# Issuing both products of a PSUM bank ahead of the bank's readers, at four places of an encoder's attention

## The chip, the cores and the metric

The kernel runs on one core of one Trainium2 chip. The metric is the device time of one execution in microseconds (us); of several executions the median is given. Matmuls run on TensorE (PE in the profile, its weight loads PEld) and write to PSUM, eight banks of 128 x 512 float32. VectorE (DVE) and ScalarE (ACT) read the banks. SyncE (SP) issues the DMAs that bring weights from HBM; GpSimd (POOL) does little here.

## The reference

Two layers work on 256 tokens of width 2048. In each, one projection of the normed and modulated input feeds two kinds of attention side by side: four heads of differential attention and eight heads of latent attention (MLA). Both results go through one output projection, and an MLP of width 8192 follows. What the change touches is this:

```python
# differential attention, per head: two score maps, softmaxes, difference, values, norm
s = einsum('bhmqd,bhmkd->bhmqk', qi, kt) * scale
p = softmax(s + bias, axis=-1)
a = p[:, :, 0] - lam * p[:, :, 1]
o = einsum('bhqk,bhkd->bhqd', a, vt)
o = _rmsnorm(o, subln_g) * (1.0 - lambda_init)
# latent attention, per head: scores are a sum of two products
s = (einsum('bhqd,bhkd->bhqk', qn, knt) + einsum('bhqr,bkr->bhqk', qr, k_rope)) * scale
o = einsum('bhqk,bhkd->bhqd', softmax(s, axis=-1), vt)
# both: out_a, out_b side by side, times w_o
```

## The kernel before

All of w_in, w_o, the MLP's weights and w_ada stream from HBM once. A weight block of 128 x 2048 (1 MB) lands in one of five `raw` buffers; ACT rounds each half to a tile `hi` (line 151) and DVE computes the rest `lo` (line 154), so that three fast products (hi by hi, hi by lo, lo by hi) stand for one full-precision product. There are four `hi` and four `lo` buffers. The blocks of w_ada share the five `raw` buffers and are consumed by one DVE instruction of 128 x 2048 (line 380). SP issues each load when a `raw` buffer comes free, that is, behind a `lo` of line 154 or a line 380.

A framework builds the program. It orders each engine's instructions by priorities and its own estimate of when each can run, and puts semaphore waits where one engine reads what another wrote, or where two engines would touch the same PSUM bank. So the order in the source decides which accesses to a bank come first, and the framework fills the gaps on PE with products of the surrounding projections.

The attention of one layer works on tokens in two halves of 128 (`t` = 0 and 1), and each of these steps puts both halves into one bank:

- `diff_probs` (line 1242): for each of two score maps `m`, a product into `psc[:, t]` (line 1249) and then at once its reader on DVE (line 1250), which adds the bias and takes the row minimum. The ACT exponentials (line 1236) follow. There are 16 such banks in the two layers.
- `mla_steps.scores` (line 1311): for each half a sum of two products in `psm[:, t]` (lines 1315 and 1316) and at once its DVE reader (line 1317). `softmax_parts` (line 1232) does both exponentials and one reciprocal (line 1239), and line 1320 scales. Then `turn` transposes the result (line 1267). There are 16 such banks.
- `diff_steps.values` (line 1273): for each half two products into `po[:, t]` (line 1280) and at once a sum of squares on ACT (line 1284). Then a square root on ACT (line 1285), a reciprocal on DVE (line 1286) and the scaling into `o` on ACT (line 1289). There are 8 such banks.
- `diff_steps.turn` (line 1292): for each of two column halves two transposes into `pot[:, d]` (line 1298), and at once ACT's `do` (line 1300) and DVE's rest of it (line 1301). There are 8 such banks.

The products of these steps are float32, which the trace shows as two passes for each matmul; the transposes are one pass. Each layer first runs the projections, with the differential scores spread over them; then the value projection with the MLA heads spread over it (lines 296 to 298 of `tokens_by_k`); then the output projection's first column block (`rows_by_k`, lines 311, 312 and 314), whose four quarters of k have the values and turned outputs of the four differential heads between them: heads 0 and 1's values ahead of the first quarter, their turned outputs and heads 2 and 3's values between the first and the second, and heads 2 and 3's turned outputs between the second and the third.

Of the kernel before, what the change touches and what calls it, by code (L numbers as in the profile page):

```python
# [101 lines left out]
class Trunk:  # L102
# [1139 lines left out]
    def diff_probs(self, l, hd, q, k):  # L1242
        nc = self.nc
        ps_, rs = [], []
        for m in range(2):
            ps = self.bank("psc")
            s, mx = self.t("s"), self.s("mx")
            for t in range(2):
                nc.tensor.matmul(ps[:, t], q[:, m, t * P : (t + 1) * P], k[:, m], start=True, stop=True)
                nc.vector.tensor_tensor_reduce(  # L1250
                    s[:, t], ps[:, t], self.bias[:, hd, t], 1.0, 3.0e38, ALU.add, ALU.min, mx[:, t : t + 1]
                )
            rs.append(self.softmax_parts(s, mx))
            ps_.append(s)
        c1 = self.s("c1")
        nc.vector.tensor_scalar(c1, rs[1], self.lam[:, l : l + 1], None, ALU.mult)
        a = self.u("a")
        for t in range(2):
            nc.vector.tensor_scalar(ps_[1][:, t], ps_[1][:, t], c1[:, t : t + 1], None, ALU.mult)
            nc.vector.scalar_tensor_tensor(a[:, t], ps_[0][:, t], rs[0][:, t : t + 1], ps_[1][:, t], ALU.mult, ALU.subtract)  # L1260
        return a
# [8 lines left out]
    def diff_steps(self, l, hd, at, v, out):  # L1270
        nc = self.nc
        st = {}

        def values():
            po = self.bank("po")
            junk, tot, r = self.t("osq"), self.s("otot"), self.s("or")
            for t in range(2):
                for kt in range(2):
                    c = (hd % 2) * 256
                    nc.tensor.matmul(  # L1280
                        po[:, t], at[hd][:, kt, t * P : (t + 1) * P], v[hd // 2][kt][:, c : c + 256],
                        start=kt == 0, stop=kt == 1,
                    )
                nc.scalar.activation(junk[:, t], po[:, t], AF.Square, accum_out=tot[:, t : t + 1])
            nc.scalar.activation(r, tot, AF.Sqrt, bias=self.eps, scale=1.0 / 256.0)
            nc.vector.reciprocal(r, r)
            o = self.t("o")
            for t in range(2):
                nc.scalar.activation(o[:, t], po[:, t], AF.Copy, scale=r[:, t : t + 1])
            st["o"] = o  # L1290

        def turn():
            o = st["o"]
            pt = self.bank("pot")
            both = [self.parts("do") for _ in range(2)]
            for d, (hi, lo, _) in enumerate(both):
                for t in range(2):
                    nc.tensor.transpose(pt[:, d, t * P : (t + 1) * P], o[:, t, d * P : (d + 1) * P], self.ident)
                g = self.gl[:, l, d : d + 1]
                nc.scalar.activation(hi, pt[:, d], AF.Copy, scale=g)  # L1300
                nc.vector.scalar_tensor_tensor(lo, pt[:, d], g, hi.bitcast(F32), ALU.mult, ALU.subtract)
            out.extend(both)

        return values, turn

    def mla_steps(self, hm, qn, qr, kn, vm):
        nc = self.nc
        st = {}

        def scores():  # L1310
            ps = self.bank("psm")
            s, mx = self.t("sm"), self.s("mxm")
            for t in range(2):
                c = slice(t * P, (t + 1) * P)
                nc.tensor.matmul(ps[:, t], qn[hm // 2][:, hm % 2, c], kn[hm // 2][:, hm % 2], start=True, stop=False)
                nc.tensor.matmul(ps[:, t], qr[hm // 4][:, (hm // 2) % 2, c], self.kr[:, hm % 2], start=False, stop=True)
                nc.vector.tensor_scalar(s[:, t], ps[:, t], -1.0, None, ALU.mult, ALU.min, accum_out=mx[:, t : t + 1])
            r = self.softmax_parts(s, mx)
            for t in range(2):
                nc.scalar.activation(s[:, t], s[:, t], AF.Copy, scale=r[:, t : t + 1])  # L1320
            st["s"] = s

        def turn():
            st["t"] = self.transposed(st["s"])

        def values():
            if hm % 2 == 0:
                self.pom = self.bank("pom")
            for kt in range(2):
                c = (hm % 4) * P  # L1330
                v = vm[hm // 4][kt].rearrange("p a b -> p (a b)")
                nc.tensor.matmul(self.pom[:, hm % 2], v[:, c : c + P], st["t"][:, kt], start=kt == 0, stop=kt == 1)
            if hm % 2:
                self.mo += self.split(self.pom, "mo", True)

        return scores, turn, values


# [91 lines left out]
```

## Time and profile before

| | us |
|---|---|
| median of 3 executions (2177.63 to 2179.71) | 2178.62 |
| the profiled execution's own time | 2180.82 |
| its span, first to last instruction | 2178.8 |
| PE busy in the span | 2147.1 (99%) |
| PEld busy | 1860.6 (85%) |
| DVE busy | 1592.7 (73%) |
| ACT busy | 1143.1 (52%) |

The granted TensorE clock was 0.998 of full speed. The table is read like this: PE has work almost all the time, so a time can only become shorter by what PE waits for, or by what its instructions take. The attention of layer 0 lies at about 160 to 335 us of the span and that of layer 1 at about 1225 to 1395 us.

### The profile page before, as it was taken

What the parts mean: (1) busy time and instruction counts of PE and PEld (TensorE: products, weight loads), DVE (VectorE), ACT (ScalarE), POOL (GpSimd) and SP (SyncE); (2) the same over time, 40 slices, a digit from 0 to 9 for tenths busy, and PEclk for the clock granted to TensorE, in tenths of its full rate; (3) what the DMA queues carried; (4) which work ended last, traced back from release to release, by engine and by line L of the source; (5) the groups of instructions that cost most, each with busy time, mean ns of one, the idle gap of its engine ahead of it and who ended that gap; (6) DMA issues with size and microseconds to landing.
All of it is one profiled execution on the core that took longest, in us unless ns stands there. A gap on an engine that the chain in (4) does not pass through costs nothing.

```text
span 2178.8 us, 29359 instructions
## 1 busy us (share of the span) xinstructions
PE 2147.1 (99%) x11502; PEld 1860.6 (85%) x11502; DVE 1592.7 (73%) x2117; ACT 1143.1 (52%) x1725; POOL 6.8 (0%) x19
## 2 busy tenths in 40 slices
PE   7999999999999999999999999999999999999998
PEld 6899878898888888888889988888888888888886
DVE  7888878888688988888876876678555555555555
ACT  6555664565455355355454565546535534644643
POOL 0000000000000000000000000000000000000000
PEclk9999999999999999999999999999999999999999
DMA  9988889799888988888967665867655554555552
GB/s 385 423 339 328 329 337 336 274 339 338 322 321 323 351 315 332 312 335 320 336 223 278 254 222 217 288 223 262 245 194 179 207 194 174 193 206 181 193 195 95
DMA packets 87243, 594.75 MB, mean 273 GB/s; under 512 B 9857, under 2 KB 10305, under 8 KB 20289
## 3 DMA queue, kind: packets, MB, share of 16 engines
q1 hardware_dynamic: 85968, 587.08, 73.2%
q0 software_dynamic: 848, 5.28, 0.7%
q8 instruction: 90, 1.47, 0.3%
q10 hardware_dynamic: 288, 0.52, 0.1%
q14 instruction: 49, 0.39, 0.1%
HBM read 589.66 MB, written 3.18 MB: 272 GB/s over the span
## 4 chain that ended last, share of the span: by engine, by line
PE 94%; DVE 2%; DMA 2%; ACT 1%; issue 0%; SPq 0%; ACTq 0%
PE ps L217 19%; PE pr L314 13%; PE pr L311 13%; PE pr L312 13%; PE ps L220 10%; PE pk L260 3%; PE pk L284 2%; PE pk L194 2%; PE pk L198 2%; PE pk L197 2%; PE pv L296 1%; PE pv L297 1%; PE pv L298 1%; DMA raw<-in_w_o 1%; PE pk L281 1%; PE ps L197 1%
## 5 line engine op out<-in xcount | busy, mean ns | idle before, releaser
L154 DVE TENSOR_TENSOR lo<-raw,hi 128x1024 fp32r<-128x1024 f32 (+1 forms) x714 | 835.6, 1193 | 441.1 <-issue 221.1
L151 ACT ACTIVATE hi<-raw 128x1024 fp32r<-128x1024 f32 (+1 forms) x714 | 733.9, 1036 | 685.8 <-PE pr L312 368.1
L380 DVE SCALAR_TENSOR_TENSOR ada<-ada,cond 128x2048 f32<-128x2048 f32 x192 | 437.9, 2284 | 12.4 <-DMA ada<-in_w_ada 11.9
L217 PE MATMUL ps<-h,hi 128*128 128x512 f32 x1856 | 431.5, 390 | 0.0
L217 PEld LDWEIGHTS ps<-h,hi 128*128 128x128 f32 x1856 | 345.1, 188 | 69.5
L311 PE MATMUL pr<-hi,hid 128*128 128x512 f32 x1024 | 398.6, 389 | 0.0
L312 PE MATMUL pr<-hi,hid 128*128 128x512 f32 x1024 | 398.5, 389 | 0.0
L314 PE MATMUL pr<-lo,hid 128*128 128x512 f32 x1024 | 253.5, 389 | 0.0
L220 PEld LDWEIGHTS ps<-h,lo 128*128 128x128 f32 x1856 | 230.3, 192 | 4.5
L220 PE MATMUL ps<-h,lo 128*128 128x256 f32 x1856 | 231.7, 283 | 0.0
L314 PEld LDWEIGHTS pr<-lo,hid 128*128 128x128 f32 x1024 | 192.3, 188 | 39.9
L312 PEld LDWEIGHTS pr<-hi,hid 128*128 128x128 f32 x1024 | 192.3, 188 | 39.7
L311 PEld LDWEIGHTS pr<-hi,hid 128*128 128x128 f32 x1024 | 192.3, 188 | 39.6
L1192 ACT ACTIVATE sum<-ps 128x256 f32<-128x256 f32 x110 | 42.0, 383 | 114.7 <-PE ps L220 114.2
L194 PE MATMUL pk<-h,hi 128*128 128x256 f32 x320 | 90.4, 285 | 0.2 <-ACT h L705 0.2
L198 PE MATMUL pk<-h,lo 128*128 128x256 f32 x320 | 90.5, 283 | 0.0
L197 PE MATMUL pk<-h,hi 128*128 128x256 f32 x320 | 90.5, 283 | 0.0
L188 DVE TENSOR_TENSOR hid<-relu,hid 128x256 fp32r<-128x256 f32 x128 | 48.3, 420 | 49.6 <-ACT hid L187 49.6
L260 PE MATMUL pk<-hf,w 128*128 128x256 f32 x384 | 83.9, 379 | 0.0
L260 PEld LDWEIGHTS pk<-hf,w 128*128 128x128 f32 x384 | 72.7, 190 | 10.0 <-ACT hf L677 0.2
L194 PEld LDWEIGHTS pk<-h,hi 128*128 128x128 f32 x320 | 61.2, 192 | 0.6 <-ACT h L705 0.5
L198 PEld LDWEIGHTS pk<-h,lo 128*128 128x128 f32 x320 | 61.4, 192 | 0.2 <-DVE lo L154 0.2
(237 smaller groups left out, 2466.6 us busy)
## 6 DMA issues: line engine op xcount, KB each, us to landing
raw<-in_w_m SPq DMA_DIRECT2D x238, 1024.0 KB, 5.2
ada<-in_w_ada SPq DMA_DIRECT2D x192, 1024.0 KB, 6.3
raw<-in_w_o SPq DMA_DIRECT2D x32, 1024.0 KB, 6.7
raw<-in_w_m SPq DMA_DIRECT2D x24, 768.0 KB, 5.6
raw<-in_w_dv SPq DMA_DIRECT2D x16, 1024.0 KB, 5.0
raw<-in_w_t SPq DMA_DIRECT2D x12, 1024.0 KB, 4.9
w<-in_w_a SPq DMA_DIRECT2D x24, 384.0 KB, 13.5
raw<-in_w_a SPq DMA_DIRECT2D x12, 768.0 KB, 5.8
```

The costliest lines, as they stand in the source:

```text
L151: ins = self.nc.scalar.activation(hi, v, AF.Copy)
L154: ins = self.nc.vector.tensor_tensor(lo, v, hi.bitcast(F32), ALU.subtract)
L194: ins = mm(ps, hi, x[0], start=first, stop=False, skip_group_check=shared)
L197: mm(ps, hi, x[1], start=False, stop=False, skip_group_check=shared)
L198: self.last_mac = mm(ps, lo, x[0], start=False, stop=last, skip_group_check=shared)
L217: mm(ps.rearrange("p a b -> p (a b)"), part(w, k, 0), x[2], start=k == 0, stop=False)
L220: mm(ps[:, 0], part(w, k, 1), x[0], start=False, stop=k == nk - 1)
L260: self.nc.tensor.matmul(ps, v, whole[k], start=first, stop=last, skip_group_check=True)
L311: mm(ps, xh[:, c], part(i, 0), start=kq == 0 and i == 0, stop=False)
L312: mm(ps, xl[:, c], part(i, 0), start=False, stop=False)
L314: self.last_mm = mm(ps, xh[:, c], part(i, 1), start=False, stop=kq == 3 and i == 3)
L380: ins = nc.vector.scalar_tensor_tensor(w, w, 1.0, self.cond, ALU.mult, ALU.mult, accum_out=acc[:, i : i + 1])
```

## The change

In all four steps the readers move out of the loop that issues the products: both halves' products come first, then both halves' readers.

```diff
@@ diff_probs
             for t in range(2):
                 nc.tensor.matmul(ps[:, t], q[:, m, t * P : (t + 1) * P], k[:, m], start=True, stop=True)
+            for t in range(2):
                 nc.vector.tensor_tensor_reduce(
                     s[:, t], ps[:, t], self.bias[:, hd, t], 1.0, 3.0e38, ALU.add, ALU.min, mx[:, t : t + 1]
                 )
@@ diff_steps, values
                         po[:, t], at[hd][:, kt, t * P : (t + 1) * P], v[hd // 2][kt][:, c : c + 256],
                         start=kt == 0, stop=kt == 1,
                     )
+            for t in range(2):
                 nc.scalar.activation(junk[:, t], po[:, t], AF.Square, accum_out=tot[:, t : t + 1])
@@ diff_steps, turn
-            for d, (hi, lo, _) in enumerate(both):
+            for d in range(2):
                 for t in range(2):
                     nc.tensor.transpose(pt[:, d, t * P : (t + 1) * P], o[:, t, d * P : (d + 1) * P], self.ident)
+            for d, (hi, lo, _) in enumerate(both):
                 g = self.gl[:, l, d : d + 1]
                 nc.scalar.activation(hi, pt[:, d], AF.Copy, scale=g)
                 nc.vector.scalar_tensor_tensor(lo, pt[:, d], g, hi.bitcast(F32), ALU.mult, ALU.subtract)
@@ mla_steps, scores
                 nc.tensor.matmul(ps[:, t], qr[hm // 4][:, (hm // 2) % 2, c], self.kr[:, hm % 2], start=False, stop=True)
+            for t in range(2):
                 nc.vector.tensor_scalar(s[:, t], ps[:, t], -1.0, None, ALU.mult, ALU.min, accum_out=mx[:, t : t + 1])
```

No instruction is added or removed; the framework orders PE, DVE and ACT anew from this, while SP's order of loads stays as it was. In the rows below line numbers above 1249 are up to four higher in the changed kernel. Names carry the number of their tile.

On PE, in layer 0 at about 230 us, where the second MLA head's scores (`psm_2166`) meet the transposes of the first head's result (`pt_2182` from `sm_2094`); `pt_2159` belongs to a differential head:

```order
-L1267 MATMUL pt_2159<-ident,a_1753 128x128 x4
-L1315 MATMUL psm_2166<-kn_1848,qn_1969 128x256
-L1316 MATMUL psm_2166<-kr_1317,qr_2045 128x256
-L1267 MATMUL pt_2182<-ident,sm_2094 128x128
+L1268 MATMUL pt_2159<-ident,a_1753 128x128 x4
+L1318 MATMUL psm_2166<-kn_1848,qn_1969 128x256
+L1319 MATMUL psm_2166<-kr_1317,qr_2045 128x256
+L1318 MATMUL psm_2166<-kn_1848,qn_1969 128x256
+L1319 MATMUL psm_2166<-kr_1317,qr_2045 128x256
+L1268 MATMUL pt_2182<-ident,sm_2094 128x128 x4
 L194 MATMUL pss_2202<-lath_1402,hi_2191 128x256
```

Both halves of the second head's scores now stand ahead of the transposes.

On DVE at the same place before, with what each row waits for (the row minima of the first MLA head, `mxm_2095`, a w_ada block, the reciprocal of the first head's sums, `r_2103`):

```order
L1317 TENSOR_SCALAR sm_2094,mxm_2095<-psm_2093 128x256 [waits PE_49]
L380 SCALAR_TENSOR_TENSOR ada_2018,macc_80<-ada_2018,cond 128x2048 [waits DMAHW3_49]
L1317 TENSOR_SCALAR sm_2094,mxm_2095<-psm_2093 128x256 [waits PE_49]
L394 TENSOR_TENSOR mod_79<-macc_80,vec 128x2 [waits DVE_49]
L154 TENSOR_TENSOR lo_2192<-raw_2189,hi_2191 128x1024 [waits DMAHW6_49,Activation_49]
L1239 RECIPROCAL r_2103<-tot_2102 128x2 [waits Activation_49]
```

And in the changed kernel:

```order
L1321 TENSOR_SCALAR sm_2094,mxm_2095<-psm_2093 128x256 [waits PE_49]
L1321 TENSOR_SCALAR sm_2094,mxm_2095<-psm_2093 128x256
L380 SCALAR_TENSOR_TENSOR ada_2018,macc_80<-ada_2018,cond 128x2048 [waits DMAHW3_49]
L1239 RECIPROCAL r_2103<-tot_2102 128x2 [waits Activation_49]
L154 TENSOR_TENSOR lo_2192<-raw_2189,hi_2191 128x1024 [waits DMAHW6_49]
```

The two readers stand together ahead of the w_ada block, the first of them carries the wait on PE for the whole bank and the second none, and the reciprocal moved ahead of a `lo`.

On PE in layer 0 between the first and the second quarter of the output projection (at about 313 to 320 us; `pot` are turned outputs of heads 0 and 1, `po` values of heads 2 and 3), before, from the last product ahead of the second visit:

```order
L311 MATMUL pr_2817<-hi_2916,mo_2775 128x512
L1298 MATMUL pot_2858<-ident,o_2792 128x128 x2
L1298 MATMUL pot_2869<-ident,o_2807 128x128 x2
L1280 MATMUL po_2880<-v_2768,aT_2164 128x256
L1280 MATMUL po_2880<-v_2770,aT_2164 128x256
```

And in the changed kernel, right behind the first quarter:

```order
L1300 MATMUL pot_2858<-ident,o_2792 128x128 x4
L311 MATMUL pr_2817<-hi_2912,mo_2672 128x512
L312 MATMUL pr_2817<-hi_2912,mo_2672 128x512
L311 MATMUL pr_2818<-hi_2912,mo_2672 128x512
L312 MATMUL pr_2818<-hi_2912,mo_2672 128x512
L311 MATMUL pr_2817<-hi_2912,mo_2673 128x512
L1300 MATMUL pot_2869<-ident,o_2807 128x128
L1281 MATMUL po_2880<-v_2768,aT_2164 128x256
L1300 MATMUL pot_2869<-ident,o_2807 128x128 x3
```

Before, thirteen products of the second quarter stood between `pot_2858`'s first two transposes and `pot_2869`; now five stand between `pot_2858` and `pot_2869`. In layer 1 the same two `pot` banks now follow each other with none between.

On ACT at that place before (`hi_2972` and `hi_2976` are the halves of the weight block for the third quarter, `or` the root, `o` the scaled output):

```order
L1289 ACTIVATE o_2792<-po_2780,or_2783 128x256
L1284 ACTIVATE osq_2796,otot_2797<-po_2795 128x256
L151 ACTIVATE hi_2972<-raw_2970 128x1024 [waits DMAHW1_49,PE_49]
L1284 ACTIVATE osq_2796,otot_2797<-po_2795 128x256 [waits PE_49]
L151 ACTIVATE hi_2976<-raw_2970 128x1024
L1285 ACTIVATE or_2798<-otot_2797,eps 128x2 [waits Activation_49]
L1300 ACTIVATE do_2859<-pot_2858,gl 128x256 [waits PE_49]
L1289 ACTIVATE o_2807<-po_2795,or_2798 128x256 [waits DVE_49]
```

And in the changed kernel:

```order
L1291 ACTIVATE o_2792<-po_2780,or_2783 128x256
L1286 ACTIVATE osq_2796,otot_2797<-po_2795 128x256 x2
L151 ACTIVATE hi_2916<-raw_2910 128x1024
L1287 ACTIVATE or_2798<-otot_2797,eps 128x2 [waits Activation_49]
L151 ACTIVATE hi_2972<-raw_2970 128x1024 [waits DMAHW1_49,PE_49]
L1291 ACTIVATE o_2807<-po_2795,or_2798 128x256 [waits DVE_49]
L1291 ACTIVATE o_2807<-po_2795,or_2798 128x256
L1303 ACTIVATE do_2859<-pot_2858,gl 128x256 [waits PE_49]
```

`o_2807` moved ahead of one of the two conversions and ahead of `do_2859`; it still stands behind `hi_2972`, which waits for a weight block to land.

## The prediction

> **What bounds the kernel now.** I read the page first, for the shares and the chain of waits:
>
> ```profile
> span 2178.8 us, 29359 instructions
> PE 2147.1 (99%) x11502; PEld 1860.6 (85%) x11502; DVE 1592.7 (73%) x2117; ACT 1143.1 (52%) x1725; POOL 6.8 (0%) x19
> PE 94%; DVE 2%; DMA 2%; ACT 1%; issue 0%; SPq 0%; ACTq 0%
> ```
>
> PE is busy 99% of the span and carries 94% of the chain that ended last. A reader on DVE or ACT costs time only where PE stands still for it. Then the table by stage, with layer 0's attention and first output columns in the first row and layer 1's in the second:
>
> ```profile
> 155.00:345.00 190.00, 184.64 (x1072) 160.82 (x1072) 163.46 (x271) 111.17 (x219) 1.18 (x2) 1.00 0.87 323
> 1215.00:1440.00 225.00, 224.59 (x1266) 194.91 (x1265) 165.23 (x269) 130.01 (x240) 1.05 (x2) 1.00 0.69 250
> ```
>
> PE (the second number) is idle 190 - 184.64 = 5.36 us in layer 0 and 0.41 us in layer 1. So the whole prize is a few us of 2179. Then PE's own waits, with what ended them:
>
> ```profile
> PE pss L194 <- ACT hi L151: 2.1, 1, 2.1
> PE pss L198 <- DVE lo L154: 1.0, 2, 0.5
> PE pot L1298 <- DVE do L1301: 1.0, 1, 1.0
> PE pt L1267 <- ACT sm L1320: 0.9, 2, 0.5
> PE po L1280 <- ACT osq L1284: 0.5, 1, 0.5
> ```
>
> The first two are for weights. The fifth and the third are a product that waits for the bank's reader. The fourth is late because the second half's product was. Those three are what the change can move.
>
> **The change part by part.** No instruction is added or removed, so each term is a wait, or a seam between two kinds of products. First the unit prices, from the timeline of PE:
>
> ```profile
> 300.22 0.39 PE L297 MATMUL pv<-lo,h 128*128 128x512 f32 x1
> 301.36 0.39 PE L296 MATMUL pv<-hi,h 128*128 128x512 f32 x1
> 304.26 2.75 PE L1280 MATMUL po<-v,aT 128*128 128x256 f32 x12
> 306.85 0.27 PE L1104 MATMUL pg<-ident,mod 128*16 128x128 f32 x1
> ```
>
> Five wide products from 300.22 to 301.36 are 0.227 us each; twelve float32 passes from 304.26 to 306.85 are 0.216.
>
> *The first MLA head's softmax, both layers.* PE, DVE and ACT in layer 0, then PE in layer 1:
>
> ```profile
> 230.38 0.60 PE L1267 MATMUL pt<-ident,a 128*128 128x128 f32 x4
> 230.82 0.60 PE L1315 MATMUL psm<-kn,qn 128*128 128x256 f32 x2
> 231.25 0.59 PE L1316 MATMUL psm<-kr,qr 128*128 128x256 f32 x2
> 232.39 0.33 PE L1267 MATMUL pt<-ident,sm 128*128 128x128 f32 x1 [0.55 <-ACT sm L1320]
> 226.97 2.28 DVE L380 SCALAR_TENSOR_TENSOR ada<-ada,cond 128x2048 f32<-128x2048 f32 x1
> 229.18 0.42 DVE L1317 TENSOR_SCALAR_CACHE_REDUCE sm<-psm 128x256 f32<-128x256 f32 x1
> 231.82 0.91 ACT L1320 ACTIVATE sm<-sm,r 128x256 f32<-128x256 f32 x2
> 1291.32 0.59 PE L1316 MATMUL psm<-kr,qr 128*128 128x256 f32 x2
> 1292.30 0.33 PE L1267 MATMUL pt<-ident,sm 128*128 128x128 f32 x1 [0.38 <-ACT sm L1320]
> ```
>
> PE's two passes from 231.25 end their turn at 231.68, and the transposes start at 232.39: 0.71 us lost; in layer 1, 1292.30 - 1291.32 - 0.43 = 0.55 us. The second reader at 229.18 stood behind a w_ada block of 2.28 us. In the new order it is ahead of the block, the reciprocal comes right behind the block, and the second head's other four passes (0.86 us) stand ahead of the transposes. So PE would ask for `sm` at 232.55 while ACT can scale it from about 230.4: both waits go, **-1.26 us**. The cover that hides what remains of this chain is those 0.86 us and the value projection ahead of it; if it is gone, the old 1.26 stay (bounds -1.26 to 0). What is moved past is the w_ada block, 0.42 us later on DVE, for which PE does not wait. The pairs of later heads show no wait on PE at all.
>
> *The last differential head in layer 0, at 203 us.*
>
> ```profile
> 202.44 1.82 PE L1249 MATMUL psc<-k,q 128*128 128x256 f32 x6
> 204.24 0.39 PE L194 MATMUL pss<-lath,hi 128*128 128x256 f32 x1
> 205.93 0.38 PE L198 MATMUL pss<-lath,lo 128*128 128x256 f32 x1 [0.51 <-DVE lo L154]
> 204.65 2.36 DVE L154 TENSOR_TENSOR lo<-raw,hi 128x1024 fp32r<-128x1024 f32 x2
> ```
>
> Six passes are 1.30 us and took 1.80 to the next product, so 0.50 is lost, and the last two passes of the second map come later. In the new order all eight passes run at once (1.73 us). But the first reader now waits for both halves (its wait on PE stands for the bank), so the first `lo`, which stands behind both readers, comes hardly earlier than at 204.65. The second `lo`, which stood directly behind the first, now has the other map's two readers ahead of it (0.42 us each, as the row at 229.18 has it for the other kind), and came only just in time at 207.01 (204.65 + 2.36). So the 0.50 won are about the 0.84 that the second `lo` comes later, less what the first gives. I take **0** (bounds -0.7 to +0.7).
>
> *Values and turned outputs in layer 0.* PE, then ACT, then the chain of waits:
>
> ```profile
> 311.31 0.84 PE L314 MATMUL pr<-lo,mo 128*128 128x512 f32 x3
> 312.69 1.13 PE L1280 MATMUL po<-v,aT 128*128 128x256 f32 x4 [0.54 <-ACT osq L1284]
> 317.12 0.39 PE L311 MATMUL pr<-hi,mo 128*128 128x512 f32 x1
> 318.49 0.82 PE L1298 MATMUL pot<-ident,o 128*128 128x128 f32 x4 [0.98 <-DVE do L1301]
> 311.43 0.84 ACT L1289 ACTIVATE o<-po,or 128x256 f32<-128x256 f32 x2 [0.26 <-DVE or L1286]
> 306.13 8.14 DMA raw<-in_w_o
> 314.35 1.06 ACT hi L151
> ```
>
> Gone: 312.69 - 311.31 - 3 x 0.227 = 0.70 and 318.49 - 317.12 - 0.23 = 1.14, together 1.84 us. Late next is the second head's `o`. PE runs 16 passes from 304.26 (to 307.7), 24 wide products (5.45, to 313.2), `pot_2858` (four transposes, 0.44 by the rows 230.38 and 230.82) and five wide products: it asks for `o` of the second head at 314.8. ACT has that behind a conversion whose block lands at 306.13 + 8.14 = 314.27, so conversion until 315.4 and half of `o` by 315.8: PE waits 1.0 us. By the same count the fourth head's `o` is about 0.3 late. Net **-0.5** (bounds: -1.84 if nothing is late; +1.6 if each of the two places waits for one more conversion of 1.06 on top of the 1.3 counted). SP's order of loads stays, but DVE's second `lo` of the second quarter waits for a conversion that is now behind `o`, about 3 us later than before, and with it the next load's issue; at that time two blocks are still on the way, which covers it.
>
> *The same in layer 1.*
>
> ```profile
> 1364.53 2.75 PE L1280 MATMUL po<-v,aT 128*128 128x256 f32 x12
> 1374.56 0.83 ACT L1289 ACTIVATE o<-po,or 128x256 f32<-128x256 f32 x2
> ```
>
> Here PE waited for nothing. Now the two `pot` banks follow each other: the first at 1364.53 + 3.46 + 5.45 = 1373.4, the second 0.44 later, at 1373.9. ACT's second `o` began at 1374.56; in the new order the two conversions of the next block stay ahead of it, and one sum of squares and the first `do` are not between them any more. I put it at 1374.0: half of it is there at 1374.4 and the rest at 1374.85, and PE's transposes, which take the halves in turn, wait some **+0.8** in all (bounds 0, and +2.1 with two more conversions of 1.06).
>
> *Seams.* Wide products behind a group of float32 passes run a little slower for a while:
>
> ```profile
> 250.67 0.59 PE L1315 MATMUL psm<-kn,qn 128*128 128x256 f32 x2
> 252.92 0.39 PE L297 MATMUL pv<-lo,h 128*128 128x512 f32 x1
> ```
>
> From 250.67 to 252.92 stand four passes and six wide products: 0.86 + 1.36 = 2.22, and it took 2.25, 0.03 us more. By the order, 47 such groups stand among the wide products of both attentions before and 25 in the changed kernel: 22 x 0.03 = **-0.7** (bounds 0, if the slower pace goes with the passes and not with the seam, and -1.5 at twice the price).
>
> Sum: -1.26 + 0 - 0.5 + 0.8 - 0.7 = **-1.7 us**. The profiled execution took 2180.82 and would take 2179.1; the median of the three runs was 2178.62, 2.2 below it, and goes to **2176.9**.
>
> A rule speaks against the change. ACT's second read of a bank that DVE reads in between shows that readers, too, take turns:
>
> ```profile
> 306.47 0.39 ACT L187 ACTIVATE mo<-pom 128x256 fp32r<-128x256 f32 x1 [0.68 <-DVE mo L188]
> ```
>
> The Trainium skill, Perfetto Trace Analysis, section Matmuls, says that independent groups of products should go to different banks in turn, so that emptying one overlaps the next group's products. By that rule a bank that is filled whole before anybody reads it gives up the overlap inside it, and the first reader starts later by the second half's products. This is the mechanism of the second rival below.
>
> **The rivals.** *All waits go and nothing comes back* (faster). For it: the three reader waits are each ended by one late reader, and the framework's own order believes `o` is ready when it puts `pot` early. Against it: the landing at 314.27 does not depend on the order of the attention. It gives -1.26 - 0.7 - 1.84 - 0 - 0.7 = -4.5: 2174.1. Chance 0.15.
>
> *Filling the bank first delays the chain behind it* (slower). The first reader of a value bank starts four passes (0.86 us) later, and ACT takes root, conversions and `o` one after the other behind it; PE now reaches the four second-of-pair `pot` banks early and waits there. It decides where `o` is more than about 1 us behind PE. The longest wait of PE for a conversion in this trace is 2.1 us (for `pss`, above); at four places that is 8.4, against 1.26 + 0.7 + 1.84 + 0.7 = 4.5 gained: +3.9, 2182.5. For it: o behind a conversion at each. Against it: in layer 1 loads land early. Chance 0.12.
>
> *The change does nothing that counts* (same). The load stream is the bound where the largest wait goes:
>
> ```profile
> 310.00:315.00 5.00, 4.46 (x21) 3.43 (x20) 3.75 (x6) 3.01 (x7) 0.49 (x1) 1.00 0.99 347
> ```
>
> DMA engines are busy 0.99 there, so what PE gains before is waited for again at the next block. Then only the MLA heads' 1.26 counts, less layer 1's 0.8: 2178.2. Against it: PE's idle time in this row, 5.00 - 4.46 = 0.54, is the wait for `osq` alone, none of it for weights. Chance 0.15.
>
> The Trainium skill, PSUM, section PSUM bank collisions raise a hardware error, has it that no two engines may touch one bank at once, readers included. The row at 306.47 agrees (0.68 us); it leaves ACT's and DVE's turns on `pot` as they are, and by it none of `pot`'s waits between those two would go.
>
> **How the numbers follow.** A change of 0.2%, 4.4 us, is about what a measurement of this kernel tells from none. The forecast has 0.58. Faster by more than 4.4 needs nearly the whole first rival: 0.08 with the forecast's tail. Slower by more needs the second rival's far end: 0.07. Same: 0.85. The range holds the forecast's bounds where one or two terms fall to an end (2.8 lower with nothing late in layer 0, 1.3, the seams' far end, 0.8, and 0.7 at 203 us; 3.4 higher with both `o` terms at their high ends, 2.1 and 1.3) and most of the rivals: 2174.0 to 2180.4.
>
> **What would show it.** In the changed profile: no wait of `pt` on `sm` and of `po` on `osq`; a wait of `pot` on ACT's `o` at about 314.8 of some 1 us, and one of under 1 us in layer 1; PE's idle time in 155 to 345 about 1 to 2 us smaller. Wrong would be: `pt` still waiting, `pot` waiting over 2 us, or new waits for weights between 330 and 400.

## The result, and the profile after

The changed kernel takes 2174.91 us (median of 14 executions, 2173.39 to 2176.31). The kernel before, run beside it, takes 2179.31 us (14 executions, 2177.63 to 2182.14). The ratio is 0.9979 with a 95% interval of 0.9971 to 0.9987: 4.4 us less, between 2.8 and 6.3. A later comparison of the same two kernels gave 0.9985 (0.9976 to 0.9994), 3.3 us less. The forecast was 1.7 us less. The sign and the range held; what follows is mostly about the 1.6 to 2.7 us that the forecast did not have.

The page of the changed kernel:

```profile
span 2172.8 us, 29358 instructions
PE 2144.7 (99%) x11502; PEld 1863.5 (86%) x11502; DVE 1590.9 (73%) x2117; ACT 1139.8 (52%) x1725; POOL 6.8 (0%) x19
```

PE's busy time fell by 2.4 us although it runs the same instructions. So a part of what went was counted as busy before. PE's own waits:

```profile
PE pss L194 <- ACT hi L151: 2.1, 1, 2.1
PE pss L198 <- DVE lo L154: 0.7, 2, 0.5
PE pr L311 <- ACT hi L151: 0.7, 2, 0.4
```

The three waits for a bank's reader (`pot` on `do`, `pt` on `sm`, `po` on `osq`) are gone. The last of these lines, the waits for blocks of `w_o`, was longer before:

```profile
PE pr L311 <- ACT hi L151: 2.4, 3, 1.0
```

These 1.7 us cannot be put down to the change: over the traces of the experiments these waits lie between 0.7 and 3.0 us, the 3.0 in a kernel with all readers behind their products and 1.0 in one whose layer 0 is that of before. The stretches of the two attentions, in the same columns as before:

```profile
155.00:345.00 190.00, 187.10 (x1077) 164.91 (x1076) 162.33 (x271) 110.07 (x219) 1.18 (x2) 0.98 0.85 322
1215.00:1440.00 225.00, 225.00 (x1267) 197.64 (x1266) 167.37 (x273) 130.21 (x243) 1.05 (x2) 1.00 0.71 254
```

PE is idle 2.90 us in layer 0 instead of 5.36, and not at all in layer 1, where it had been idle 0.41. By this table layer 1 can have given no more than 0.41 us. Two fixed points say otherwise. They are the first product of layer 0's MLP and the first of layer 1's; between them lies all of layer 1's attention. Timeline of PE before:

```profile
410.75 0.62 PE L194 MATMUL pk<-h,hi 128*128 128x256 f32 x3 [0.24 <-ACT h L705]
1465.67 0.62 PE L281 MATMUL pk<-h,lo 128*128 128x256 f32 x3 [0.24 <-ACT h L705]
```

And in the changed kernel:

```profile
407.79 0.62 PE L194 MATMUL pk<-h,hi 128*128 128x256 f32 x3 [0.24 <-ACT h L705]
1459.86 0.62 PE L281 MATMUL pk<-h,lo 128*128 128x256 f32 x3 [0.24 <-ACT h L705]
```

This stretch took 1054.92 us and now takes 1052.07, **2.85 us less**. Layer 1, for which my terms sum to about nothing (-0.55 + 0.8 - 0.3), gave more than half of the whole gain. The two profiled executions differ by 6.1 us, more than the medians do; of that, 3.0 us lie ahead of the first point (410.75 to 407.79) and 0.2 us behind the second.

**What the busy share hid.** Here is one place in layer 1 before the change, at the first half and second half of one score bank; all engines, rows of ACT and of other instructions left out:

```profile
1236.72 0.40 DVE L1250 CUSTOM_DVE_ANT_0 s<-psc,bias 128x256 f32<-128x256 f32 x1
...
1236.89 0.28 PE L198 MATMUL ps<-h,lo 128*128 128x256 f32 x1
1237.05 0.08 DVE L1250 DVE_READ_ACCUMULATOR2_ANT mx<- 128x1 f32 x1
1237.18 0.30 PEld L1249 LDWEIGHTS psc<-k,q 128*128 128x128 f32 x2 [0.21 <-DVE mx L1250]
1237.18 0.70 PE L1249 MATMUL psc<-k,q 128*128 128x256 f32 x2
...
1237.53 0.47 PE L194 MATMUL ps<-h,hi 128*128 128x256 f32 x1
...
1237.84 0.28 PE L197 MATMUL ps<-h,hi 128*128 128x256 f32 x1
```

The fast products (`ps`) start every 0.12 us. The product after 1236.89 was due at 1237.01 and started at 1237.18: its weights could be loaded only once the first half's reader had ended, at 1237.05 + 0.08 = 1237.13. From 1237.18 to 1237.84 stand two passes (0.43) and one fast product (0.12), 0.55, and it took 0.66. The wait cost 0.17 + 0.11 = 0.28 us. PE's row carries no idle time for it, because the bar of the product at 1236.89 is 0.28 long, more than the 0.12 from one start to the next, and covers the gap. PEld's row does carry it, 0.21. The same place in the changed kernel, PE:

```profile
1236.62 1.89 PE L1249 MATMUL psc<-k,q 128*128 128x256 f32 x8
1238.16 0.47 PE L194 MATMUL ps<-h,hi 128*128 128x256 f32 x1
1238.47 0.28 PE L197 MATMUL ps<-h,hi 128*128 128x256 f32 x1
```

Eight passes and one fast product from 1236.62 to 1238.47 are 1.85 us, exactly 8 x 0.216 + 0.12.

So the view that I should have read is the table of waits of PEld, here for 1215 to 1440 us before:

```profile
PEld psm L1315 <- DVE sm L1317: 0.9, 4, 0.3
PEld po L1280 <- ACT osq L1284: 0.9, 3, 0.3
PEld pqr L1222 <- ACT qr L346: 0.8, 1, 0.8
PEld pt L1267 <- ACT sm L1320: 0.8, 1, 0.8
PEld pt L1267 <- issue: 0.5, 2, 0.3
PEld pot L1298 <- ACT o L1289: 0.4, 2, 0.2
PEld psc L1249 <- ACT k L346: 0.2, 1, 0.2
PEld psc L1249 <- DVE mx L1250: 0.2, 1, 0.2
```

And of the changed kernel:

```profile
PEld pqr L1222 <- ACT qr L346: 0.8, 1, 0.8
PEld pt L1268 <- issue: 0.5, 2, 0.3
```

Of these waits PE's own view held one, `pt` on `sm`. The table tells which reader was waited for, and not what it cost: `psc` has 0.4 us in it, of two waits, and by the starts of the products lost 1.14 us; `psm` has 0.9 and lost 0.50. The Trainium skill, Perfetto Trace Analysis, section Identifying the Most-Contended Engine, says that the busy share of matmuls is not a good measure of how close a kernel is to its roofline, because matmuls are pipelined, and names the busy share of the weight loads as one of two to use instead. This case agrees: with PE at 224.59 of 225.00 us busy before, and 225.00 after, the stretch between the fixed points still became 2.85 us shorter, while PEld's busy time went from 194.91 to 197.64.

To compare all kernels I summed, from the starts of PE's passes, what each entry into and step inside a group (products of one kind that follow each other) took beyond its pace (0.216 us for a pass, 0.109 for a transpose), in layer 1. The last column is the stretch between the two fixed points.

| kernel | `psc` | `psm` | `pt` | `po` | `pot` | stretch |
|---|---|---|---|---|---|---|
| before, two traces | 1.14, 1.15 | 0.50, 0.51 | 0.56, 0.57 | 0.48, 0.48 | 0.11, 0.12 | 1054.92, 1054.86 |
| changed, two traces | 0.09, 0.09 | 0.00, 0.00 | 0.01, 0.01 | 0.00, 0.00 | 0.01, 0.01 | 1052.07, 1052.08 |

Layer 1 repeats to 0.1 us from one execution to the next. Layer 0 does not, as the experiments show.

### The profile page after: what moved, and what is told of

Read it like the earlier page. It is cut to its first block, busy times and chain, and to the rows that moved or that the text cites. A ratio compares the mean times of both kernels' runs of the same rounds, so it can differ in the third digit from the quotient of the medians.

```text
span 2172.8 us, 29358 instructions
## 1 busy us (share of the span) xinstructions
PE 2144.7 (99%) x11502; PEld 1863.5 (86%) x11502; DVE 1590.9 (73%) x2117; ACT 1139.8 (52%) x1725; POOL 6.8 (0%) x19
## 4 chain that ended last, share of the span: by engine, by line
PE 97%; DVE 2%; DMA 1%; ACT 0%; SPq 0%; issue 0%; ACTq 0%
PE ps L217 19%; PE pr L312 13%; PE pr L311 13%; PE pr L314 13%; PE ps L220 10%; PE pk L260 3%; PE pk L284 2%; PE pk L194 2%; PE pk L198 2%; PE pk L197 2%; PE pv L298 2%; PE pv L296 2%; PE pv L297 2%; PE pk L281 1%; PE ps L198 1%; PE ps L197 1%
```

## The experiments

Theory A: the gain out of sight is short waits of a bank's second product on the first one's reader. Theory B: it is the groups of other products, of which the changed kernel has fewer, each at a price. Later runs ask which layer the gain lies in.

**One part at a time.** Each of four kernels has one of the four edits of the diff and nothing else.

```diff
@@ diff_probs (first kernel)
+            for t in range(2):
                 nc.vector.tensor_tensor_reduce(...)
@@ mla_steps, scores (second kernel)
+            for t in range(2):
                 nc.vector.tensor_scalar(s[:, t], ps[:, t], -1.0, ...)
@@ diff_steps, values (third kernel)
+            for t in range(2):
                 nc.scalar.activation(junk[:, t], po[:, t], AF.Square, ...)
@@ diff_steps, turn (fourth kernel)
+            for d in range(2):
+                for t in range(2):
+                    nc.tensor.transpose(pt[:, d, ...], o[:, t, ...], self.ident)
             for d, (hi, lo, _) in enumerate(both):
```

> Only the differential scores (psc) get both products ahead of the readers; the rest is as before. Theory A, short waits: in the trace of before the first pass of a bank's second half starts 0.05 us after the first half's reader ends, and it and the pass behind it take 0.1 to 0.3 us longer than passes elsewhere; the table of waits does not list these. Summed over the start-to-start times of PE they are 0.5 us in layer 0 and 1.06 us in layer 1. A expects these sums to fall to under 0.1 each and the time to fall by 1.6 us to about 2177.7. Theory B, seams: the same time was lost at each change between kinds of products; layer 1 lost 2.05 us more than its one listed wait, over 28 groups that are fewer in the changed kernel, 0.073 us each. Here 15 groups go: -1.1 us, 2178.2, with the short waits of psm, po and pot smaller too if they belong to groups. Theory C, my prediction's own account: nothing at 203 us and 0.03 a seam, -0.45 us, 2178.9.

> Only the MLA scores (psm) get both products ahead of the readers. Both A (short waits) and my prediction expect the two waits of pt on sm to go, 0.71 us in layer 0 and 0.55 us in layer 1. A adds the short waits of psm, 0.1 us in layer 0 and 0.5 us in layer 1: -1.85 in all, 2177.5. B (seams at 0.073 us, 16 groups fewer) gives -1.26 - 1.17 = -2.4: 2176.9. The prediction's price of 0.03 gives -1.26 - 0.48 = -1.74. The traces should tell: under A the entries into psm cost nothing any more while entries into psc, po and pot cost what they did.

> Only the values (po) get both products ahead of the squares. A: the listed wait on osq in layer 0 (0.70 us and 0.10 for the pass behind it) and short waits of 0.17 in layer 0 and 0.48 in layer 1 go, -1.4 us in all; in layer 0 part of it may be waited for again at weights at 375 us. 2177.9. B: 3 groups fewer at 0.073 and the listed wait: -0.9. The prediction's mechanism of a late o would show as a longer wait of pot.

> Only the turned outputs (pot) are issued ahead of their readers. A: the listed wait on do in layer 0 (1.14 us) and some 0.3 us of short waits go, and as nothing of the values moves, the second head's o is as late as before, so pot waits for o: by the prediction 1.0 us in layer 0. So A expects -0.5 to -1.4: 2177.9 to 2178.8. If pot does not wait for o, the prediction's term of +1.3 in layer 0 was wrong without the values' help; if it does, the change of the values is what keeps o in time in the full change.

Measured against before (2178.95, 33 executions), and in layer 1 of the trace:

| only | time, us | ratio (95%) | `psc` | `psm` | `pt` | `po` | `pot` | stretch, less than before |
|---|---|---|---|---|---|---|---|---|
| `psc` | 2177.85 | 0.9992 (0.9983 to 1.0001) | 0.09 | 0.51 | 0.56 | 0.45 | 0.12 | 1.06 |
| `psm` | 2177.74 | 0.9994 (0.9985 to 1.0003) | 1.14 | 0.00 | 0.01 | 0.44 | 0.12 | 1.26 |
| `po` | 2177.94 | 0.9994 (0.9985 to 1.0003) | 1.17 | 0.51 | 0.56 | 0.01 | 0.22 | 0.40 |
| `pot` | 2179.40 | 1.0001 (0.9992 to 1.0010) | 1.16 | 0.51 | 0.56 | 0.29 | 0.24 | 0.17 |

None of the four is told from no change by its time. By the medians each gave less than A expected (1.1 us for 1.6, 1.2 for 1.85, 1.0 for 1.4, and 0.4 more for 0.5 to 1.4 less); their sum is 2.9 us less. The traces tell them apart. Each edit takes away the waits of its own kind and leaves the others: with `psc` alone, PEld's waits in 1215 to 1440 us are these, all of before but the two on `psc`:

```profile
PEld psm L1316 <- DVE sm L1318: 0.9, 4, 0.3
PEld po L1281 <- ACT osq L1285: 0.9, 3, 0.3
...
PEld pt L1268 <- ACT sm L1321: 0.8, 1, 0.8
...
PEld pot L1299 <- ACT o L1290: 0.4, 2, 0.2
```

With `psm` alone, `psm` and `pt` are gone and the rest stands:

```profile
PEld po L1280 <- ACT osq L1284: 0.9, 3, 0.3
...
PEld pot L1298 <- ACT o L1289: 0.4, 2, 0.2
PEld psc L1249 <- ACT k L346: 0.2, 1, 0.2
PEld psc L1249 <- DVE mx L1250: 0.2, 1, 0.2
```

The four stretches sum to 2.89 us against 2.85 for the whole change, so in layer 1 the parts add up. Theory A gave 1.06 for `psc` and got 1.06. In layer 0 the second head's `o` was late for `pot` with the values alone (PE waited 0.3 us for it), and not with the turned outputs alone, against my expectation. In layer 1 the edit of the turned outputs is worth little by itself, and it does not stand alone: with `po` batched and `pot` not, `pot` waits for `do` (0.22 instead of 0.11), and only both together bring it to 0.01. In layer 1 each of the two edits of the scores leaves eight groups fewer, so B's 0.073 us a group would have given `psc` and `psm` 0.58 us each beside `pt`; without `pt` the stretches give 1.06 and 0.70, and the single places lose 0.08 to 0.28 each, which is no one price for each group.

**Groups back, waits not.** The changed kernel, with the second halves' products issued later but still ahead of both readers:

```diff
@@ tile_cols
             self.mac(ps, w[k // per], (k % per) * m, m, xs[k], k == 0, k == nk - 1)
+            if k in (3, 6) and self.held:
+                self.held.pop(0)()
@@ diff_probs: the products of t = 0 at once; held (heads 0 to 2), one for each map:
+            product(m, 1)
             for t in range(2):
                 nc.vector.tensor_tensor_reduce(...)
```

> The changed kernel, but the second half's differential scores (psc) of heads 0 to 2 are issued three and six blocks into the next column, still ahead of both readers. PE then has 10 groups of psc in layer 1 instead of 4 (and 6 instead of 4 in layer 0), as before the change, but no product waits for a reader of its own bank. A (short waits on the first half's reader): a seam without such a wait costs nothing; the sum of what PE loses at the entries into psc in layer 1 stays at 0.1 us as in the changed kernel, where it was 1.14 us with the readers between, and the time stays at that of the changed kernel, about 2174.9. B (seams at 0.073 us): layer 1 gets 0.44 us longer and layer 0 0.15. My prediction's price of 0.03 would give 0.18 and 0.06.

The sum for `psc` in layer 1 is 0.12 us, the stretch 1052.06, and the time 2175.03 (0.9984, 0.9976 to 0.9993) beside 2175.57 for the changed kernel on the same chip. Six more groups in layer 1 cost 0.03 us together, where theory B gives 0.44 and my price of 0.03 for each 0.18: both are refuted. (The trace is of a long execution, 2178.97 us. What made it long lies ahead of the stretch; in layer 0 PE waited 3.0 us for blocks of `w_o`.)

**The wait taken away by another bank.** The order of the source as before, a bank for each half:

```diff
@@ diff_probs
-            ps = self.bank("psc")
             s, mx = self.t("s"), self.s("mx")
             for t in range(2):
+                ps = self.bank("psc")
@@ mla_steps, scores: the same with "psm"
```

> The kernel before, readers in their old place in the source, but each half of psc and of psm has a bank of its own, so the second product has no reader to wait for. po and pot as before. A: the same waits go as with the two changes of the scores alone: in layer 1 psc from 1.14 to 0.1, psm from 0.50 to 0, pt from 0.56 to 0, 2.3 us together (1.07 and 1.27 by those two runs from the same point to the same point), po and pot unchanged at 0.6. If it is not the wait on the bank but the place of the readers on VectorE that counts (both behind both products, ahead of a block of w_ada), psc and psm keep part of their loss here. If filling a bank before anybody reads it costs something, this kernel is faster than those two runs together, since its first reader starts a product earlier.

`psc` 0.09, `psm` 0.00, `pt` 0.01, `po` 0.44, `pot` 0.13; the stretch is 2.13 us shorter, against 1.06 + 1.26 = 2.32 for the two single edits. The time is 2176.23 (0.9987, 0.9978 to 0.9995). Of PEld's waits in the changed steps in layer 1, those on `po` and `pot` alone are left:

```profile
PEld po L1280 <- ACT osq L1284: 0.9, 3, 0.3
...
PEld pot L1298 <- ACT o L1289: 0.4, 2, 0.2
```

So what counted is that the second product had to wait for a reader of its own bank. Where the readers stand matters little: of `psc`, `psm` and `pt` together 2.1 us went here, as in the two single edits. A first reader that may start a product earlier brings nothing either, since the stretch did not become shorter than those two give. That it is 0.2 us longer than their sum shows in no wait of the table. My prediction held against the change a rule of the Trainium skill (Perfetto Trace Analysis, section Matmuls: let independent groups go to different banks). Both ways of keeping that wait away, two banks or one bank filled first, take away the same waits of the scores here; for the scores, filling one bank first has cost nothing that a run shows.

**Both kernels once more.**

> The kernel before once more, for a second trace. Layer 1 should repeat to 0.1 us: psc 1.14, psm 0.50, pt 0.56, po 0.48, pot 0.11 us. Layer 0 is the question: in the first trace PE waited 2.4 us for halves of w_o between 375 and 395 us, in the traces of the single parts only 0.7 to 1.0. If that belongs to the execution and not to the kernel, this trace has about 1 us there too, and the 3 us by which layer 0 differed between the first two traces were partly chance.

> The changed kernel once more, beside the others on one chip, and a second trace. About 2174.9 us. Layer 1 should repeat to 0.1 us; in layer 0, what PE waits for weights may change by a microsecond either way.

The kernel before took 2178.72 us in one execution, the changed one 2175.57 (ratio to before 0.9985, 0.9976 to 0.9994). Layer 1 repeats, as the table above shows. Layer 0 does not: from the last product of the setup, at 83 us, to the first of the MLP it took 327.43 and 325.83 us before, and 324.47 and 321.89 in the changed kernel. My expectation was not met: what PE lost to waits for halves of `w_o` between 345 and 410 us is the same 3.1 us in the second trace of before. (The kernel with the edits in layer 1 alone, below, whose layer 0 is that of before, lost 1.4 there, so it does vary.) What changed between the two traces is what my prediction counted as gone, the waits of PEld in 155 to 345 us. The first trace of before:

```profile
PEld pot L1298 <- DVE do L1301: 1.8, 2, 1.4
...
PEld po L1280 <- ACT osq L1284: 1.0, 1, 1.0
```

And the second:

```profile
PEld po L1280 <- ACT osq L1284: 0.4, 1, 0.4
PEld pot L1298 <- DVE do L1301: 0.4, 1, 0.4
```

Some two thirds of these two waits, 2.0 of 2.8 us, belonged to that one execution. The 2.6 us between the two traces of the changed kernel are of another kind, the clock of PE (last section).

**One layer at a time.** All four edits, in one layer only:

```diff
                 nc.tensor.matmul(ps[:, t], q[:, m, t * P : (t + 1) * P], k[:, m], start=True, stop=True)
+                if l != BATCHED:
+                    read(t)
+            if l == BATCHED:
+                for t in range(2):
+                    read(t)
@@ the same at psm, po and pot; BATCHED = 0 or 1
```

> All four edits, but in layer 0 alone; layer 1 is issued as before. In the traces so far layer 1 loses exactly as much each time (3.2 and 3.1 us in two traces of before, 0.36 in both of the changed kernel), while what layer 0 loses between 155 and 410 us varies by 1.4 us between two traces of before and by 2.7 between two of the changed kernel. A (short waits, and a load stream that sets layer 0): the change as a whole is 3.3 to 4.4 us by three comparisons, of which 2.8 are layer 1's, so layer 0's share is 0.5 to 1.6: about 2177.9. My prediction's own account (all the gain in layer 0, -1.6) gives 2177.3 here and no gain in the next run.

> All four edits, but in layer 1 alone; layer 0 is issued as before. A: -2.8 us from the start of layer 0's MLP to that of layer 1's, and the same in the time: about 2176.1. By the terms of my prediction layer 1 alone would give -0.55 for the MLA head, +0.8 for the turned outputs and -0.3 for seams: no change, 2178.9.

Layer 1 alone: 2175.79 us against 2179.22, ratio 0.9987 (0.9978 to 0.9996), and the stretch is 1052.11 us, 2.8 less:

```profile
408.53 0.62 PE L195 MATMUL pk<-h,hi 128*128 128x256 f32 x3 [0.24 <-ACT h L706]
1460.64 0.62 PE L282 MATMUL pk<-h,lo 128*128 128x256 f32 x3 [0.24 <-ACT h L706]
```

Layer 0 alone: 2177.96 us, ratio 0.9994 (0.9985 to 1.0003), and the stretch is unchanged at 1054.84:

```profile
408.11 0.61 PE L195 MATMUL pk<-h,hi 128*128 128x256 f32 x3 [0.24 <-ACT h L706]
1462.95 0.62 PE L282 MATMUL pk<-h,lo 128*128 128x256 f32 x3 [0.24 <-ACT h L706]
```

Layer 1's part is settled: 2.8 us, from the waits in the table. Layer 0's part is 1.3 us by this comparison, with an interval that reaches from 3.3 less to 0.7 more, so it is not told from nothing by itself. From 83 to 410 us the three traces with layer 0 as before took 327.43, 325.83 and 325.27 us, and the three with all four edits in it 324.47, 321.89 and 324.59. All of the second group are shorter, but each group spreads by 2 to 3 us, so the sign is likely and the size stays open. The trace of layer 0 alone also shows the new wait that I had forecast, PEld in 155 to 345 us:

```profile
PEld pot L1322 <- ACT o L1306: 1.9, 2, 1.1
```

**The best without its weakest part.** The changed kernel without the edit of the turned outputs:

> The changed kernel without its edit of the turned outputs (pot), the one part that showed no gain by itself. In layer 1 the edits of psc, psm and po give 2.76 of 2.85 us by their own runs, so layer 1 should be within 0.2 us of the changed kernel's. In layer 0 pot waits less for o where its transposes are not batched. I expect 2175 to 2176, no difference from the changed kernel that can be measured; if it is more than 1 us faster, pot's edit costs something in layer 0.

2175.68 us (0.9986, 0.9977 to 0.9995), the stretch 1052.36, 0.3 more than the changed kernel's. That is a little more than I expected, and in time nothing that can be measured. In layer 1 the trace speaks for keeping the edit. Whether it pays in layer 0 is not shown: without it `pot` lost 0.19 us there, with it 0.20 in both traces of the changed kernel, but over 1.2 in two other kernels.

## Why the prediction was right in its range and wrong in its sum

- **What bounds the kernel.** That readers cost time only where PE stands still was right. Taking PE's idle time (5.36 us and 0.41 us) as "the whole prize" was the failing step: waits of up to 0.28 us lie under the bars of the products ahead of them. In layer 1, 2.7 us of waits went where I read 0.41 us of idle time. I had counted 0.55 of them, by the starts (`pt`); to `psc`, `psm` and `po` of layer 1 I gave nothing because of that step.
- **The first MLA head, -1.26.** Right: `pt` lost 0.73 us in layer 0 and 0.56 in layer 1 and now loses 0.01 in each. The same edit also took 0.1 us and 0.50 us of short waits at `psm`, which I had at zero ("show no wait on PE at all").
- **203 us, 0.** Inside its bounds: between 202 and 211 us PE lost 1.40 us by the starts in both traces of before, and 1.04 and 1.05 in those of the changed kernel. Over all of layer 0 the entries into `psc` lost 0.61 and 0.96 us in two traces and lose 0.09. In layer 1, where I gave this edit nothing, it is 1.06 us, more than any one kind of wait there.
- **Values and turned outputs in layer 0, -0.5.** The mechanism held, its size belongs to the execution. Of the 1.84 us gone, less than half was there in the second trace of before, where `po` and `pot` lost 0.41 and 0.37 us by the starts. The late `o` of the second head, which I had named as the sign to look for, was all but absent in both traces of the changed kernel (`pot` lost 0.20), and there in two other kernels with these edits in layer 0 (1.23 and 1.45 us). It goes with the landing of the block ahead of it: I had counted with the 8.14 us of the first trace; in the changed kernel the block took 6.4 and 6.6 us from its issue, in the other two 7.3 and 7.5.
- **The same in layer 1, +0.8.** Wrong. PE and ACT of the changed kernel, from the start of the eight transposes of both banks:

```profile
1368.40 1.03 PE L1300 MATMUL pot<-ident,o 128*128 128x128 f32 x8
```

```profile
1364.98 0.39 ACT L1286 ACTIVATE osq<-po 128x256 f32<-128x256 f32 x1
...
1366.83 1.07 ACT L151 ACTIVATE hi<-raw 128x1024 fp32r<-128x1024 f32 x1
1367.78 0.85 ACT L1291 ACTIVATE o<-po,or 128x256 f32<-128x256 f32 x2
```

  The second bank's transposes start 0.44 us into the row, at 1368.84, and `o` is done at 1368.63. I had taken ACT's `o` from its old time and only subtracted what no longer stood between. But its squares came earlier too, since the product that they wait for no longer waited for the first square. In place of +0.8 the values and turned outputs of layer 1 gave -0.6 (0.48 and 0.11).
- **Seams, -0.7.** Wrong in cause: six groups more cost 0.03 us, and no run shows a price for each group. So 0.7 us of the forecast came from something that did not happen.
- **The rivals.** The first, all waits go and nothing comes back, came nearest in time (-4.5), but by other terms: it counts 1.84 us that were partly chance, and it has none of the 2.3 us that layer 1 lost out of sight. The second needed `o` late at four places; two places in layer 0 were late in some executions, none in layer 1. The third is refuted for layer 1, whose 2.85 us were not waited for again. For layer 0 it stays open: PE's waits for `w_o` vary by more (0.7 to 3.0 us) than the share in question.
- **Luck.** That the time fell inside the range is in part luck. The range's lower end was made of nothing late in layer 0, of 0.7 us at 203 us and of seams at twice their price. The seams did not come about, and nothing in the range stood for the 2.3 us that layer 1 lost out of sight.

## What to carry to other kernels

Find PE's waits in the table of its weight loads and take their cost from start to start, not from the idle time between products: waits of up to 0.28 us left no gap here. Where two products share a bank and a reader of the first stands between them, the second can become a short wait even where the view of PE shows none, and here some fifteen such places of one layer summed to 2.1 us; issue both products first, or give each its bank. When one instruction's place is costed, move its inputs as well before taking its old time as a base.

## What the runs showed that I had not expected

At the place in layer 1 shown above, the weight load that had waited starts 0.05 us after the reader's end (1237.13 to 1237.18), and not only it but the pass behind its own is late: the pair took 0.11 us more than two passes and a product at pace.

PE's granted clock fell after the 2.1 us wait for weights at 211 us, in some executions only. The changed kernel at 215 to 220 us, first trace and second:

```profile
215.00:220.00 5.00, 5.00 (x24) 5.00 (x25) 5.00 (x4) 0.00 (x0) 0.00 (x0) 0.50 0.61 223
215.00:220.00 5.00, 4.67 (x39) 4.67 (x40) 5.00 (x5) 1.25 (x2) 0.00 (x0) 1.00 0.55 175
```

The fast products started 0.21 us apart in the first instead of 0.12. In four of thirteen traces, both of before and the second of the changed kernel among them, the clock in this slice was 1.00; in the other nine it was 0.50 to 0.72, with the same wait ahead of it. From 205 to 228 us the steps from one fast product to the next took 2.7 us more in the first trace than in the second, which is all of the 2.6 us by which layer 0 differs between the two. PE's busy share shows none of it: the slower slice is the one with 5.00 of 5.00 us busy.
